# Fifteen projections of a two-layer hybrid decoder: three 256-column matmuls become one of 512 and one of 256, with some small TensorE work put together

## The chip, the cores and the metric

The kernel runs on one NeuronCore of a Trainium2 chip, in one launch. The metric is the device time of that launch in microseconds. The kernel before takes 1352.6 us, the median of three runs (1352.0 to 1353.1).

## The reference

Two layers, each `x <- LayerNorm(alpha * x + mixer(x))`, on x of 256 positions by 2048 channels, all in float32. Layer 0 has one input projection whose columns feed a Mamba-2 SSD mixer (xs, z, B, C, dt) and a block-sparse attention (q, k, v, gate); with 256 positions there is one block of 256 keys, so the attention is plain causal attention. Layer 1 is an S5 mixer: a projection to u and a gate, a diagonal complex scan over positions, a GLU, an output projection.

```python
def ssd_moba_mixer(x, w_in, ...):
    z, xbc, dt, q, k, v, gate = jnp.split(x @ w_in, SPLITS0, axis=-1)
    xbc = jax.nn.silu(causal_depthwise_conv(xbc, conv_w, conv_b))
    xs, bm, cm = jnp.split(xbc, ...)
    y = ssd_chunked_scan(xh * dt[..., None], dt * a, bm, cm)
    y = y + d_skip[:, None] * xh
    y_a = rms_norm(y * jax.nn.silu(z), norm_g)
    y_b = moba_attention(rope(q), rope(k), v) * jax.nn.silu(gate)
    return jnp.concatenate([y_a, y_b], axis=-1) @ w_out

def s5_mixer(x, w_in, ...):
    u, gate = jnp.split(x @ w_in, 2, axis=-1)
    y = jax.nn.gelu(s5_ssm(u, ...))          # scan over positions, 128 groups of 16 channels
    ga, gb = jnp.split(y @ w_glu, 2, axis=-1)
    return (ga * jax.nn.sigmoid(gb) * jax.nn.silu(gate)) @ w_out
```

## The kernel before

**Products.** Every large product is made from fp32r matmuls (one pass over float32 operands of reduced precision). To keep float32 accuracy each operand is split in a high and a low part, x = xh + xl and w = wh + wl, and three terms are summed in PSUM: wh·xh, wh·xl and wl·xh. The activations lie in SBUF as `xh` and `xl`, [128, 16 k-tiles, 256 positions], in slots called A and B (later C and F). The weights are streamed: one unit is 512 KB in a `raw` tile (two k-tiles of 512 columns, `_chunk`, L90). `split_to` (L209) issues its DMA on the SP queue, makes wh on ACT (L230) and wl on DVE (L232); four buffers of each, so a unit is split up to three units ahead of the one TensorE works on. A product of 512 output columns over 2048 rows is `CU` = 8 units.

**Two kinds.** `product` (L301) has kind "x", where a 128x128 piece of x is stationary and 512 weight columns move (`xmm`, L271, the matmul is L276), and kind "w", where a 128x128 piece of the weight is stationary and the 256 positions of x move (`wmm`, L280, the matmul is L297). Kind "w" leaves the output transposed (channels on partitions), which the conv, z, q, k, the gates and u need. A product owns two PSUM banks (`banks`, L267), and two products alternate between two pairs. In a "w" product the 512 output columns are four tiles of 128 (index o), two in each bank, and every tile takes three 256-column matmuls per k-tile (i = 0, 1, 2 in L297).

**The order of work.** After each unit, `pump` (L248) runs some of `jobs` (what the last product left to do) and of `back` (long-running work, spread over a number of units by `goal`). `run` (L242) places a job behind the weight split two units ahead, and a scheduler settles the order of each engine's queue when the program is built. Each engine then works in order. The products follow each other so: B and C together, xs (4 products), z (4), then four times q, k, v, gate, then the output projection of layer 0, u (4), the S5 gate (4), the GLU, the output projection.

**The work around the change.**
- `conv_jobs` (L523): for each tile of 128 channels one ACT operation and three DVE operations (L532) that read the product in PSUM, into an SBUF tile; then SiLU.
- z: SiLU on ACT from PSUM into `sz` (slot D), two jobs for each product (L853). The attention gates: the same into `sg`, L957. u: `u_store` (L1101) copies PSUM to the SBUF tile `ut` on ACT and sends it to DRAM on the POOL queue, from where the scan loads it again.
- `head_jobs` (L774): the SSD sums, for pairs of heads k = 0..15, in five steps: bcast (two TensorE matmuls, L782), decay (ACT), weigh (DVE), apply (TensorE, L812 and L813, float32, into half of a PSUM tile that two pairs share), comb (DVE, ACT, POOL). `skewed` runs step s of pair k in round k + s, the late steps first, so each round has the apply of one pair and the bcast of another.
- `block_jobs` (L662): the tables of the S5 scan, 16 blocks, as `back` work from v of the first head group on: bars, efs, fcs on DVE, `pes` (L709) with four transposes (L715) and eight small float32 matmuls (L719) on TensorE, and for every second block `mts` (L734).

Of the kernel before, what the change touches and what calls it, by code (L numbers as in the profile page):

```python
# [16 lines left out]
P = 128  # L17
S = 256
# [3 lines left out]
CU = KT // UK  # L22
ALPHA = 4.0 ** 0.25
# [70 lines left out]

def _layout(inp):
# [12 lines left out]
    cols = [xs, z]  # L108
    for h in range(4):
        cols += [m[:, 512 * h : 512 * h + 512] for m in (q, k, v, g)]  # L110
    b, c = _chunk(b), _chunk(c)
    first = np.stack([b[:PAIRED], c[:PAIRED]], 1).reshape(-1, P, UK * 512)
    a["wi0"] = np.concatenate([first, b[PAIRED:], c[PAIRED:]] + [_chunk(m) for m in cols], 0)
# [4 lines left out]
    a["wi1"] = _chunk(f["in1_w"][0])  # L118
# [44 lines left out]
def trunk(tc, io, out):  # L163
# [8 lines left out]
    with ExitStack() as top:  # L172
# [98 lines left out]
        def xmm(ps, o, wpair, j, hk, start, stop):  # L271
            (xh, xl), k = hk
            wh, wl = wpair
            sl = slice(o * P, o * P + P)
            for i, (l, r) in enumerate(((xh, wh), (xh, wl), (xl, wh))):
                T.matmul(ps[o], l[:, k, sl], r[:, j, :], start=start and i == 0, stop=stop and i == 2)  # L276
# [3 lines left out]
        def wmm(ps, u, nu, hl, wpair, parts=WHOLE):  # L280
            pv = [p.rearrange("p (f n) -> p f n", n=S) for p in ps]
            wh, wl = wpair
            for part in parts:
# [7 lines left out]
                for j, o in steps:  # L291
                    first, end = u == 0 and j == 0, u == nu - 1 and j == UK - 1
                    (xh, xl), k = hl(u * UK + j)
# [7 lines left out]
        def product(kind, hl, nu=CU, prelude=None, first=WHOLE):  # L301
# [15 lines left out]
            return ps  # L317

# [73 lines left out]
        xh = big("A", [P, KT, S], F32R)  # L392
        xl = big("B", [P, KT, S], F32R)
# [10 lines left out]
        with ExitStack() as l0:  # L404
# [35 lines left out]
            def xhl(k):  # L440
                return (xh, xl), k
# [81 lines left out]
            def conv_jobs(ps, ft, dst):  # L523
                acc = a4([P, 4, S])

                def tap(f):
                    def go():
                        src = ps[f // 2][:, (f % 2) * S : (f % 2) * S + S]
                        A.activation(acc[:, f, :], src, AF.Identity, bias=cb[:, ft + f : ft + f + 1], scale=cw[:, ft + f, 3:4])
                        for k in (2, 1, 0):  # L530
                            sh = 3 - k
                            V.scalar_tensor_tensor(acc[:, f, sh:], src[:, : S - sh], cw[:, ft + f, k : k + 1], acc[:, f, sh:],  # L532
                                                   op0=OP.mult, op1=OP.add)
# [11 lines left out]
            fmem = big("F", [P, 4096])  # L545
# [114 lines left out]
            ktp = [None]  # L660

            def block_jobs(b):  # L662
# [3 lines left out]
                def bars():  # L666
                    bc = h["bc"] = pp.tile([P, 4, 8, 16], F32, tag="bc", name=nm("bc"))
                    nc.sync.dma_start(bc.rearrange("p a g m -> p (a g m)"), io["s5bc"][b].rearrange("p a g m -> p (a g m)"))
                    bb = h["bb"] = pp.tile([P, 3, 8, 16], F32, tag="bb", name=nm("bb"))
# [10 lines left out]
                    V.tensor_scalar(bb[:, 2], bc[:, 2], nsg, None, op0=OP.mult)  # L680
# [7 lines left out]
                def efs():  # L688
                    bc, bb = h["bc"], h["bb"]
                    et = h["et"] = pp.tile([P, 8, 16, 4], F32, tag="et", name=nm("et"))  # L690
# [18 lines left out]
                def pes():  # L709
                    et, ob, bb = h["et"], h["ob"], h["bb"]  # L710
                    ev = et.rearrange("p (a i) m s -> p a (i m s)", i=2)
                    cv = bb[:, 2].rearrange("p (a i) m -> p a i m", i=2)
                    pe, pk = aux(), aux()
                    for a in range(4):
                        T.transpose(pe[:, a * P : a * P + P], ev[:, a, :], ident)  # L715
                    for a in range(4):
                        for i in range(2):
                            at = 64 * (i ^ (a % 2))
                            T.matmul(pk[at : at + 64, a * 16 : a * 16 + 16], ev[:, a, 64 * i : 64 * i + 64], cv[:, a, i, :], start=True, stop=True)  # L719
                    A.activation(ob[:, 0:512], pe, AF.Copy)  # L720
                    if b % 2 == 0:
                        ktp[0] = pp.tile([P, 8, 16], F32, tag="kt", name=nm("kt"))
                    kt = ktp[0][:, 4 * (b % 2) : 4 * (b % 2) + 4, :]
                    dc = PR("s5d")[:, 4 * b : 4 * b + 4].unsqueeze(2).to_broadcast([P, 4, 16])
                    V.tensor_tensor(kt, C("kmask").unsqueeze(1).to_broadcast([P, 4, 16]), dc, op=OP.mult)
                    V.tensor_tensor(kt, pk[:, 0:64].rearrange("p (a m) -> p a m", m=16), kt, op=OP.add)
                    nc.scalar.dma_start(wb[b][:, 0:1024], ob)
# [14 lines left out]
                return [bars, efs, fcs, pes, mts] if b % 2 else [bars, efs, fcs, pes]  # L742

            xs = big("C", [P, 2, D])
# [19 lines left out]
            for j in range(4):  # L764
                ps = product("w", xhl)
                xs_jobs(ps, j)

            sz = big("D", [P, KT, S])
# [5 lines left out]
            def head_jobs(k):  # L774
# [40 lines left out]
                def comb():  # L815
                    if k % 2 == 1:
                        sv = sz[:, k - 1 : k + 1, :].rearrange("p f n -> p (f n)")
                        V.tensor_tensor(sv, d["y"], sv, op=OP.mult)
                        jk = c2([P, 2, S])
                        A.activation(jk.rearrange("p f n -> p (f n)"), sv, AF.Square)  # L820
                        for f in range(2):
                            G.tensor_tensor(ssq, ssq, jk[:, f, :], op=OP.add)

                return [bcast, decay, weigh, apply, comb]
# [24 lines left out]
            for j in range(4):  # L849
                ps = product("w", xhl)  # L850
                for i in range(2):
                    fs = slice(4 * j + 2 * i, 4 * j + 2 * i + 2)
                    jobs.append(lambda ps=ps, i=i, fs=fs: A.activation(sz[:, fs, :].rearrange("p f n -> p (f n)"), ps[i], AF.Silu))  # L853
# [24 lines left out]
            def attn_jobs(g, qT, kT, v, sg):  # L878
                for hp in range(2):
# [37 lines left out]
                    def pv(hp=hp, hold=hold):  # L917
# [8 lines left out]
                        if not yb:  # L926
                            yb["h"] = big("C", [P, KT, S], F32R)
                            yb["l"] = big("F", [P, KT, S], F32R)
# [9 lines left out]
            for g in range(4):  # L938
# [9 lines left out]
                if g == 0:  # L948
# [6 lines left out]
                ps = product("w", xhl)  # L955
                sg = a4([P, 4, S])
                jobs.extend([lambda ps=ps, sg=sg, i=i: A.activation(sg[:, 2 * i : 2 * i + 2, :].rearrange("p f n -> p (f n)"), ps[i], AF.Silu)  # L957
                             for i in range(2)])
                attn_jobs(g, qT, kT, v, sg)

            yah = big("A", [P, KT, S], F32R)
            yal = big("B", [P, KT, S], F32R)
# [11 lines left out]
            def mixhl(k):  # L974
                if k < 12:
                    return (yb["h"], yb["l"]), k
                if k < 28:
                    return (yah, yal), k - 12
                return (yb["h"], yb["l"]), k - 16

            def tailhl(k):
                return ((yb["h"], yb["l"]), k) if k < 16 else ((yah, yal), k - 16)
# [30 lines left out]
        with ExitStack() as lt:  # L1013
# [22 lines left out]
            def turned(t, f0, nf):  # L1036
                if not x1t:
                    x1t["h"] = big("C", [P, KT, S], F32R)
                    x1t["l"] = big("F", [P, KT, S], F32R)
# [42 lines left out]
            def x1hl(k):  # L1082
                return (x1t["h"], x1t["l"]), k
# [6 lines left out]
        with ExitStack() as l1:  # L1090
# [10 lines left out]
            def u_store(ps, j):  # L1101
                ut = w1("ut", [P, 4, S], 1)
                for i in range(2):
                    A.activation(ut[:, 2 * i : 2 * i + 2, :].rearrange("p f n -> p (f n)"), ps[i], AF.Copy)
                nc.gpsimd.dma_start(ud[j].rearrange("g a c -> (g a c)").rearrange("(f p t) -> p f t", p=P, t=S), ut)
# [115 lines left out]
            def y_split(j):  # L1221
                if j == 0:
                    y5["h"] = big("A", [P, KT, S], F32R)
                    y5["l"] = big("B", [P, KT, S], F32R)
# [23 lines left out]
            def y5hl(k):  # L1248
                return (y5["h"], y5["l"]), k

            y2h = big("C", [P, KT, S], F32R)
            y2l = big("F", [P, KT, S], F32R)
# [24 lines left out]
            def y2hl(k):  # L1277
                return (y2h, y2l), k
# [7 lines left out]
        with ExitStack() as l2:  # L1286
            tp = l2.enter_context(tc.tile_pool(name="tp2", bufs=1))
            keep[0], keep[1] = tp, range(unit[0] + 2 * CU, unit[0] + 3 * CU)
            gb1 = big("A", [P, 2, D])
# [55 lines left out]
```

## Time and profile before

| what | time or share |
|---|---|
| median of 3 runs | 1352.6 us |
| the profiled execution, its own time | 1355.75 us |
| its span, first to last instruction | 1353.9 us |
| ACT_TABLE_LOAD of one ACT group in it | 1283 ns each |
| HBM read / written | 260.41 MB / 20.97 MB |
| mean DMA rate over the span | 208 GB/s |

The profile's page has the busy time of each engine, the span in 40 slices, the DMA queues, the chain of work that ended last and the costliest groups of instructions. A matmul's recorded length is modelled and runs on into the next ones, so on TensorE (PE) the distance from one start to the next is what counts; the weight loads (PEld) run beside the matmuls. Other views list who waited for whom, the instructions in order of time, and the engines' busy time in stretches of the span.

### The profile page before, as it was taken

The numbers are of one execution on the slowest core, as the hardware profiler recorded it, in microseconds if no ns is written. First come the engines' busy times: TensorE is split into PE (matmuls) and PEld (weight loads), VectorE is DVE, ScalarE is ACT, GpSimd is POOL, SyncE is SP. The second block draws the span as 40 slices with busy tenths as digits, with TensorE's granted clock in tenths as the row PEclk, the third lists the DMA queues.
The fourth block names the chain that finished last, engine by engine and source line by source line (L and its number), as shares of the span: only waits on it lengthen the run. The fifth ranks groups of instructions, "written<-read, shape, count | busy, mean of one in ns | idle before, by whom it ended". The sixth has DMA issues, their size and how long they took to land.

```text
span 1353.9 us, 24904 instructions
## 1 busy us (share of the span) xinstructions
PE 1337.0 (99%) x9839; PEld 1205.5 (89%) x9839; DVE 981.2 (72%) x1560; ACT 673.0 (50%) x870; POOL 364.8 (27%) x648
## 2 busy tenths in 40 slices
PE   9999999999999999999999999999999999999996
PEld 8999999998998998998988888899988888888885
DVE  5767856787687879689787766748889856555556
ACT  5566567764544553554554334334444545444441
POOL 0041000122026528616798500022343100000001
PEclk9999999999999999999999999999999999999998
DMA  8655555545546756856767778497989766666762
GB/s 313 192 171 176 173 171 158 157 143 178 175 135 207 254 163 203 269 160 206 232 206 243 232 232 302 136 300 223 318 275 326 217 211 189 187 196 188 250 214 81
DMA packets 80741, 283.01 MB, mean 209 GB/s; under 512 B 9840, under 2 KB 12528, under 8 KB 80112
## 3 DMA queue, kind: packets, MB, share of 16 engines
q1 hardware_dynamic: 68112, 239.33, 56.2%
q0 software_dynamic: 7328, 30.42, 6.5%
q10 hardware_dynamic: 5184, 11.67, 2.3%
q8 instruction: 77, 1.26, 0.4%
q14 instruction: 40, 0.33, 0.1%
HBM read 260.41 MB, written 20.97 MB: 208 GB/s over the span
## 4 chain that ended last, share of the span: by engine, by line
PE 93%; DVE 4%; DMA 2%; issue 1%; ACT 0%; POOL 0%; SPq 0%; POOLq 0%; ACTq 0%; DVEq 0%
PE main L276 43%; PE main L297 42%; DVE wl L232 1%; PE aux L381 1%; PE aux L812 1%; PE aux L719 1%; PE enc L1149 1%; DMA bc<-in_s5bc 1%; PE dec L1194 1%; PE aux L924 1%; PE aux L892 1%; DMA ud<-ut 0%; PE aux L782 0%; PE dec L1190 0%; PE aux L715 0%
## 5 line engine op out<-in xcount | busy, mean ns | idle before, releaser
L232 DVE TENSOR_TENSOR wl<-raw,wh 128x1024 fp32r<-128x1024 f32 x431 | 538.4, 1251 | 323.4 <-ACT wh L230 317.4
L230 ACT ACTIVATE wh<-raw 128x1024 fp32r<-128x1024 f32 x431 | 455.8, 1059 | 580.3 <-PE main L276 269.2
L297 PE MATMUL main<-A,wh 128*128 128x256 f32 x1408 | 400.7, 285 | 1.3 <-ACT wh L230 1.1
L297 PE MATMUL main<-B,wh 128*128 128x256 f32 x1408 | 398.0, 284 | 0.0
L297 PE MATMUL main<-A,wl 128*128 128x256 f32 x1408 | 394.5, 283 | 0.0
L297 PEld LDWEIGHTS main<-A,wh 128*128 128x128 f32 x1408 | 269.7, 192 | 3.0 <-ACT wh L230 1.3
L297 PEld LDWEIGHTS main<-B,wh 128*128 128x128 f32 x1408 | 269.8, 192 | 0.4
L297 PEld LDWEIGHTS main<-A,wl 128*128 128x128 f32 x1408 | 267.8, 192 | 0.2 <-issue 0.2
L276 PE MATMUL main<-wl,A 128*128 128x512 f32 x512 | 200.5, 392 | 0.5 <-DVE wl L232 0.5
L276 PE MATMUL main<-wh,A 128*128 128x512 f32 x512 | 200.5, 392 | 0.0
L276 PE MATMUL main<-wh,B 128*128 128x512 f32 x512 | 199.9, 390 | 0.0
L276 PE MATMUL main<-wh,C 128*128 128x512 f32 x384 | 150.7, 393 | 0.0
L276 PE MATMUL main<-wh,F 128*128 128x512 f32 x384 | 149.8, 390 | 0.0
L276 PE MATMUL main<-wl,C 128*128 128x512 f32 x384 | 149.7, 390 | 0.0
L276 PEld LDWEIGHTS main<-wl,A 128*128 128x128 f32 x512 | 96.2, 188 | 21.3 <-DVE wl L232 1.8
L276 PEld LDWEIGHTS main<-wh,B 128*128 128x128 f32 x512 | 96.2, 188 | 19.9
L276 PEld LDWEIGHTS main<-wh,A 128*128 128x128 f32 x512 | 96.1, 188 | 19.8 <-issue 0.2
L653 POOL TENSOR_TENSOR c<-c 128x8 f32<-128x8 f32 (+2 forms) x192 | 106.7, 574 | 25.5 <-DMA wb<-c 18.0
L276 PEld LDWEIGHTS main<-wh,F 128*128 128x128 f32 x384 | 72.1, 188 | 15.3
L276 PEld LDWEIGHTS main<-wh,C 128*128 128x128 f32 x384 | 72.1, 188 | 15.1
L276 PEld LDWEIGHTS main<-wl,C 128*128 128x128 f32 x384 | 72.1, 188 | 14.6
L873 POOL TENSOR_TENSOR a<-a,b 64x512 f32<-64x512 f32 x16 | 28.2, 1769 | 169.1 <-DVE b L872 132.1
(279 smaller groups left out, 1651.6 us busy)
## 6 DMA issues: line engine op xcount, KB each, us to landing
raw<-in_wi SPq DMA_DIRECT2D x271, 512.0 KB, 4.0
raw<-in_wo SPq DMA_DIRECT2D x96, 512.0 KB, 4.3
raw<-in_wglu SPq DMA_DIRECT2D x64, 512.0 KB, 3.6
wt<-wb POOLq DMA_DIRECT2D x16, 896.0 KB, 6.9
wb<-ob ACTq DMA_DIRECT2D x16, 512.0 KB, 5.8
bc<-in_s5bc SPq DMA_DIRECT2D x16, 256.0 KB, 4.6
wb<-c POOLq DMA_DIRECT2D x16, 256.0 KB, 3.4
wb<-om ACTq DMA_DIRECT2D x16, 128.0 KB, 4.3
```

The source lines that it names most:

```text
L230: high = A.activation(wh, raw, AF.Copy)
L232: splits[n] = (loaded[-1], high, V.tensor_tensor(wl, raw, wh.bitcast(F32), op=OP.subtract))
L276: T.matmul(ps[o], l[:, k, sl], r[:, j, :], start=start and i == 0, stop=stop and i == 2)
L297: T.matmul(pv[o // 2][:, o % 2, :], l[:, j, sl], r[:, k, :], start=first and i == 0 and o % 2 == 0, stop=end and i == 2 and o % 2 == 1, sk ...
L381: end = T.transpose(dst[:, i * P : i * P + P], s, ident)
L653: G.tensor_tensor(p[:, :, :, 0:m], cs[:, :, :, 1 : m + 1], cs[:, i, :, n : n + 1].unsqueeze(1).to_broadcast([P, 2, 4, m]), op=OP.mult)
L719: T.matmul(pk[at : at + 64, a * 16 : a * 16 + 16], ev[:, a, 64 * i : 64 * i + 64], cv[:, a, i, :], start=True, stop=True)
L812: T.matmul(yo, xs[:, 0, xc], df[:, i, 0:256], start=True, stop=False)
L873: turns.append(G.tensor_tensor(q[0:64], q[0:64], tm, op=OP.add))
L892: T.matmul(px[:, 128:384], qT[:, h, P:S], kT[:, h, :], start=True, stop=True)
L924: T.matmul(po, v[:, 0, hs], pT[:, i, 0:256], start=True, stop=False)
L1149: T.matmul(px[64 * at : 64 * at + 64, i, r * 128 + q * 64 : r * 128 + q * 64 + 64], wt[64 * i : 64 * i + 64, a * P + 64 * r : a * P + 64 * ...
```

## The change

A new function, `product_wide`, takes the place of `product("w", ...)` for xs, z, the four attention gates and u products 1 to 3 (15 products). The high and low x now lie side by side in one tile, [128, 16, 2, 256] (`duo`), so that one matmul of 512 moving columns multiplies wh by both; its two halves of the PSUM bank hold wh·xh and wh·xl. A second matmul of 256 columns adds wl·xh to the second half. A bank then holds one tile of 128 channels, so a product runs in two halves of 256 output columns, each with two banks and four units; the weights of these products are laid out in units of four k-tiles of 256 columns (`_half`). At the end of each half, `total` copies the first half of the bank to SBUF on ACT and adds the second half on DVE, for each of two tiles. The SiLU of z and the gates then works in place on 1024 columns in SBUF, one job for a product; the taps of xs read the sum in SBUF (in `sz`, which z overwrites later); u is stored from the sum. q, k, B, C, the first u product and all of kind "x" keep their matmuls.

The slots A and B become one tile, and so do C and F (the table of C·B for the SSD sums, in F before, takes the upper half of C). Two smaller parts: the apply of an even head pair moves one round later, into the round of the odd pair's apply, and the rounds between have bcast alone; `pes` runs for two blocks at once (eight transposes, then sixteen small matmuls, and one set of two DVE operations instead of two).

```diff
+def _half(w):
+    k, n = w.shape
+    return w.reshape(k // (HK * P), HK, P, n // S, S).transpose(3, 0, 2, 1, 4).reshape(-1, P, HK * S)
...
+        def product_wide(hl, dst, then):
+            for h in range(2):
+                ps = banks()
+                for u in range(HU):
+                    split_to(unit[0] + 3)
+                    wh, wl = (w.rearrange("p a n -> p (a n)").rearrange("p (k n) -> p k n", k=HK) for w in ready.pop(unit[0]))
+                    steps = [(j, o) for o in range(2) for j in range(HK)] if u == HU - 1 else [(j, o) for j in range(HK) for o in range(2)]
+                    for j, o in steps:
+                        first, end = u == 0 and j == 0, u == HU - 1 and j == HK - 1
+                        (xh, xl, xx), k = hl(u * HK + j)
+                        sl = slice(o * P, o * P + P)
+                        T.matmul(ps[o], wh[:, j, sl], xx[:, k, :, :].rearrange("p a n -> p (a n)"), start=first, stop=False, skip_group_check=True)
+                        T.matmul(ps[o][:, S : 2 * S], wl[:, j, sl], xh[:, k, :], start=False, stop=end, skip_group_check=True)
+                    unit[0] += 1
+                    pump(2 * HU - 1 - HU * h - u)
+
+                def total(o, ps=ps, h=h):
+                    to = dst()[:, 2 * h + o, :]
+                    A.activation(to, ps[o][:, 0:S], AF.Copy)
+                    V.tensor_tensor(to, to, ps[o][:, S : 2 * S], op=OP.add)
+
+                for o in range(2):
+                    run(lambda o=o: total(o))
+                then(h)
...
+        def duo(tag):
+            t = big(tag, [P, KT, 2, S], F32R)
+            return t[:, :, 0, :], t[:, :, 1, :], t
...
                 def pes():
...
+                    pair = [(b - 1, pend.pop()), (b, h)]
+                    pk = aux()
...
+                    for n, (k, d) in enumerate(pair):
+                        pe = aux()
...
+                        transpose4(pe, [ev[:, a, :] for a in range(4)])
+                        A.activation(d["ob"][:, 0:512], pe, AF.Copy)
+                        nc.scalar.dma_start(wb[k][:, 0:1024], d["ob"])
+                    for n, (k, d) in enumerate(pair):
...
+                                T.matmul(pk[at : at + 64, 64 * n + a * 16 : 64 * n + a * 16 + 16], d["ev"][:, a, 64 * i : 64 * i + 64], cv[:, a, i, :], start=True, stop=True)
...
-                return [bars, efs, fcs, pes, mts] if b % 2 else [bars, efs, fcs, pes]
+                return [bars, efs, fcs, pes, mts] if b % 2 else [bars, efs, fcs, lambda: pend.append(h)]
...
             for j in range(4):
-                ps = product("w", xhl)
-                xs_jobs(ps, j)
+                raw = sz[:, 4 * j : 4 * j + 4, :]
+                product_wide(xhl, lambda raw=raw: raw, lambda h: None)
+                xs_jobs(raw, j)
...
-                return [bcast, decay, weigh, apply, comb]
+                return [bcast, decay, weigh, apply, comb] if k % 2 else [bcast, decay, weigh, lambda: None, apply]
...
-                ps = product("w", xhl)
-                for i in range(2):
-                    fs = slice(4 * j + 2 * i, 4 * j + 2 * i + 2)
-                    jobs.append(lambda ps=ps, i=i, fs=fs: A.activation(sz[:, fs, :].rearrange("p f n -> p (f n)"), ps[i], AF.Silu))
+                zs = sz[:, 4 * j : 4 * j + 4, :]
+                product_wide(xhl, lambda zs=zs: zs, lambda h, zs=zs: jobs.append(lambda: A.activation(zs, zs, AF.Silu)) if h else None)
...
-                ps = product("w" if j < 4 else "x", x1hl) if j else first1
-                if j < 4:
-                    jobs.append(lambda ps=ps, j=j: u_store(ps, j))
+                if j in range(1, 4):
...
+                    product_wide(x1hl, ut, lambda h, ut=ut, j=j: jobs.append(lambda: u_store(ut(), j)) if h else None)
+                    continue
+                ps = product("x", x1hl) if j else first1
```

More of the change, by code (lines that the diff above doesn't have):

```diff
@@ L22 @@
 CU = KT // UK
+HK = 4
+HU = KT // HK
 ALPHA = 4.0 ** 0.25
@@ L720, in pes @@
[L720 to L726, printed above, removed]
@@ L954, in trunk @@
                     goal[0] = unit[0] + 13 * CU + 6 * CU
-                ps = product("w", xhl)
                 sg = a4([P, 4, S])
-                jobs.extend([lambda ps=ps, sg=sg, i=i: A.activation(sg[:, 2 * i : 2 * i + 2, :].rearrange("p f n -> p (f n)"), ps[i], AF.Silu)
-                             for i in range(2)])
+                product_wide(xhl, lambda sg=sg: sg, lambda h, sg=sg: jobs.append(lambda: A.activation(sg, sg, AF.Silu)) if h else None)
                 attn_jobs(g, qT, kT, v, sg)
-            yah = big("A", [P, KT, S], F32R)
-            yal = big("B", [P, KT, S], F32R)
+            yah, yal, yax = duo("A")
             def ya_job(i):
```

114 lines of the change are left out of this document (61 added, 53 removed).

## The prediction

> **What bounds the kernel now.** I read the page first, then the waits, then the chain of work that ended last, then single stretches in order of time. The page:
>
> ```profile
> span 1353.9 us, 24904 instructions
> PE 1337.0 (99%) x9839; PEld 1205.5 (89%) x9839; DVE 981.2 (72%) x1560; ACT 673.0 (50%) x870; POOL 364.8 (27%) x648
> ...
> PE 93%; DVE 4%; DMA 2%; issue 1%; ACT 0%; POOL 0%; SPq 0%; POOLq 0%; ACTq 0%; DVEq 0%
> ```
>
> TensorE is busy 99% of the span and holds 93% of the chain. Its busy time alone proves little, since recorded matmuls overlap, so I look at what it waits for (who waited for whom, TensorE's rows; us, times, longest):
>
> ```profile
> PE main L297 <- DVE F L1048: 1.3, 1, 1.3
> PE enc L1149 <- DMA um<-ud: 1.3, 1, 1.3
> PE main L297 <- ACT wh L230: 1.1, 1, 1.1
> ...
> PE main L276 <- DVE wl L232: 0.5, 2, 0.3
> ```
>
> No wait is over 1.3 us. The weight splits, the heaviest work of DVE, make it wait 0.5 us in the whole run. TensorE's stream is the bound, and a nanosecond taken from it counts in full until something else is late.
>
> **The wide products.** The chain of waits has long stretches of one kind of matmul (start, us, what):
>
> ```profile
> 148.06 23.03 PE main L297 x192
> ...
> 1155.37 21.81 PE main L276 x96
> ```
>
> 256 columns take 23.03/192 = 0.1199 us, 512 columns 21.81/96 = 0.2272 us. Doubling the columns adds 0.1073 us, so each matmul pays 0.1199 - 0.1073 = 0.0126 us whatever its width. Before, a k-tile and a tile of 128 channels cost 3 x 0.1199 = 0.3597 us; after, 0.2272 + 0.1199 = 0.3471 us. The columns streamed stay 768: what goes is one fixed part. It is tempting to read 22% off a change from three matmuls to two, or off the chain's shares; the row gives 3.5%. There are 15 products x 16 k-tiles x 4 tiles = 960 such triples: 960 x 0.0126 = **12.1 us**.
>
> Before has no stream that alternates 512 and 256 columns. The nearest alternation is the dt product, 256 columns with weights of 64 and 32 columns by turns, 32 matmuls from the first row here to the last:
>
> ```profile
> 75.60 0.28 PE L453 MATMUL aux<-A,wdp 128*64 128x256 f32 x1
> 75.71 0.28 PE L454 MATMUL aux<-B,wdp 128*32 128x256 f32 x1
> ...
> 79.26 0.28 PE L297 MATMUL main<-A,wl 128*128 128x256 f32 x1
> ```
>
> (79.26 - 75.60)/32 = 0.1144 us for 256 columns. If the short matmul of the new pair ran so, the pair would be 0.3416 us and the gain 960 x 0.0181 = 17.4 us. At the other end the pair takes as long as the triple and the gain is nothing; a loss I exclude, since every column and every weight load that stays was there before. I take 12.1: the weights here are 128 columns wide, as in the 23.03 us row, and a matmul's spacing in both rows holds one weight load for each matmul, as in the new stream.
>
> The Trainium skill (TensorE: Matmul & The Clock Gate, Back-to-back issue gap) gives a warm matmul N/2.4 + 2.5 ns, 109 ns for 256 columns and 216 for 512; dropping one of three would then be worth 2.5 ns, an estimate of 2.4 us in all, where the rows here (120 and 227 ns) make it 12.1. The rows decide, but the page speaks against this change, and it returns as a rival.
>
> **The sums after each half.** Each of 60 tiles adds an ACT copy and a DVE addition of 256 columns. Prices from the groups:
>
> ```profile
> L1263 DVE TENSOR_TENSOR p<-main,gt 128x256 f32<-128x256 f32 x16 | 6.0, 415 | 0.5 <-ACT gt L1261 0.5
> ...
> L788 ACT ACTIVATE b<-aux,cums 128x256 f32<-128x256 f32 x32 | 15.0, 469 | 0.4 <-POOL a L873 0.4
> ```
>
> DVE gets 60 x 0.415 = 24.9 us, ACT 60 x 0.469 = 28.1 us, less the copies and SiLUs that now read sums (u's copies fall away for three products). Taps that read SBUF instead of PSUM: the nearest rows are
>
> ```profile
> L532 DVE SCALAR_TENSOR_TENSOR a<-main,params,a 128x255 f32<-128x255 f32 x24 | 10.9, 467 | 1.6 <-ACT a L529 1.6
> ...
> L795 DVE SCALAR_TENSOR_TENSOR b<-b,dts,F 128x256 f32<-128x256 f32 x32 | 16.7, 522 | 0.0
> ```
>
> so 48 taps may cost up to 48 x 0.055 = 2.6 us more on DVE. None of this is TensorE's. The cover is DVE's idle time in each product. The stretches of the fullest wide products (z 0, u 2, u 3; then one unchanged v for comparison; after the length: busy PE, PEld, DVE, ACT, POOL):
>
> ```profile
> 153.70:177.60 23.90, 23.90 (x202) 23.90 (x202) 22.59 (x57) 12.21 (x15) 0.00 (x0) 1.00 0.58 177
> ...
> 621.60:644.60 23.00, 23.00 (x118) 19.00 (x117) 22.81 (x39) 10.29 (x11) 13.45 (x25) 1.00 0.75 237
> ...
> 919.70:946.60 26.90, 26.90 (x387) 26.30 (x386) 23.20 (x34) 11.11 (x12) 9.24 (x17) 1.00 0.76 234
> 946.60:972.70 26.10, 26.10 (x355) 25.70 (x354) 21.91 (x32) 10.37 (x13) 11.49 (x20) 1.00 0.89 301
> ```
>
> A product gets 4 x 0.415 = 1.7 us of DVE and 64 x 0.0126 = 0.8 us less of TensorE. u 2: 24.9 of 26.1, u 3: 23.6 of 25.3; both fit. z 0: 24.3 of 23.1, 1.2 us too much; but the splits run three units ahead, 3 x 8 x 0.347 = 8.3 us, so a backlog of 1.2 us is not seen. The v stretch shows that DVE at 22.81 of 23.00 did not stop TensorE. The sum waits for TensorE's last matmul of the tile, and behind it in ACT's and DVE's queue stand the split of the unit three ahead and the last product's jobs. That split needs the buffer of the very unit that ends the half, so it could not start much earlier. The banks are wanted again four units later, 11 us. Still the queues get fuller: I put 1 us of new waits on TensorE, between 0 (everything covered) and 6 (0.1 us for each of 60 sums).
>
> **The larger rounds.** A visit of float32 matmuls costs more than its columns: entering, and going back to fp32r. bcast alone, then an apply visit, then two products of attention in one visit:
>
> ```profile
> 198.90 0.28 PE L297 MATMUL main<-A,wl 128*128 128x256 f32 x1
> 199.02 0.39 PE L782 MATMUL aux<-cumhl,sel 128*128 128x256 f32 x2
> 199.25 0.28 PE L297 MATMUL main<-A,wh 128*128 128x256 f32 x1
> ```
>
> ```profile
> 308.19 0.28 PE L297 MATMUL main<-A,wl 128*128 128x256 f32 x1
> 308.39 0.66 PE L812 MATMUL aux<-b,C 128*64 128x256 f32 x4
> 308.88 0.40 PE L813 MATMUL aux<-b,C 128*64 128x128 f32 x4
> 309.20 0.39 PE L297 MATMUL main<-A,wh 128*128 128x256 f32 x1
> 309.43 0.28 PE L297 MATMUL main<-B,wh 128*128 128x256 f32 x1
> ```
>
> ```profile
> 479.23 0.60 PE L924 MATMUL aux<-b,a 128*128 128x256 f32 x2
> 479.66 0.38 PE L925 MATMUL aux<-b,a 128*128 128x128 f32 x2
> 479.88 0.60 PE L924 MATMUL aux<-b,a 128*128 128x256 f32 x2
> ```
>
> bcast alone costs 199.25 - 198.90 - 0.12 = 0.23 us and needs no way back (sel and cumhl are fp32r). An apply visit costs 309.43 - 308.19 - 0.24 = 1.00 us, 0.11 of it behind the first matmul of main. A second apply in the same visit is the same columns as the attention pair, 479.88 - 479.23 = 0.65 us. Each apply put into another's visit saves 0.35 us. In the order in which the changed program issues its matmuls, visits with an apply go from 17 to 10: 7 x 0.35 = **2.5 us**. The tables:
>
> ```profile
> 403.75 0.28 PE L297 MATMUL main<-A,wl 128*128 128x256 f32 x1
> 403.87 0.60 PE L715 MATMUL aux<-consts,et 128*128 128x128 f32 x4
> 404.39 0.64 PE L719 MATMUL aux<-bb,et 128*64 128x16 f32 x16
> 404.97 0.39 PE L297 MATMUL main<-A,wh 128*128 128x256 f32 x1
> 405.19 0.28 PE L297 MATMUL main<-B,wh 128*128 128x256 f32 x1
> ```
>
> A visit is 405.19 - 403.75 - 0.24 = 1.20 us. Two in one save the way back of one; that is at least the 0.10 us behind the first main matmul and at most the 0.35 of the apply. I take 0.3, nearer the apply because here too the tile sizes change twice: 8 x 0.3 = **2.4 us**. Against it: after each attention gate there is now one SiLU job instead of two, so the two scores that shared a pump fall into two, four visits more in that order. At 0.25 each (inside the same bounds) that is **1.0 us**.
>
> **The sum**, against the profiled execution's own 1355.75 us, which is 3.15 over the median of the runs: -12.1 - 2.5 - 2.4 + 1.0 + 1.0 = -15.0, so 1340.75 there, **1337.6** as a median.
>
> **The rivals.**
> - *The fixed part stays* (chance 0.13): the next wide matmul's weights load under the short one, and if that load sets the pace the pair takes as long as the triple. For it: no row shows the mixture. Against it: in the 23.03 us row each load hides under 0.12 us. Without the 12.1 us: 1352.6 - 2.9 = 1349.7. The skill's gap above would end at the same place, an estimate of 1347.3.
> - *The short matmul runs at the dt product's pace* (0.12): 17.4 instead of 12.1 us, 1332.3. Against it: the weights there are narrow.
> - *DVE gets late in part* (0.09): in the order of the queues the sums push splits back where DVE is above 0.94 of a stretch. At 0.1 us for each of 60 sums, 6 us in place of 1: 1342.6.
> - *The sums become the bound* (0.07), the slower side: at the 30 ends of halves the lead of 8.3 us is gone, because DVE comes into them with a backlog, and TensorE stands for a copy and an addition, 0.469 + 0.415 = 0.88 us, each time: +26.5 instead of +1, 1363.1. It is slower than before from 16/30 = 0.53 us an end. Against it: 0.5 us of waits for wl in the whole run, and a v stretch at 0.99 without a stop.
>
> **How the numbers follow.** Forecast 0.59. Its own range, with 8 to 16 us for the pairs' part (inside 0 to 17.4) and 2 to 4 for the rounds: 1333 to 1343. To leave out no more than 2 in 10 it reaches to both neighbours: 1329 (17.4 us of pairs, 5 of rounds, no waits: 1330.2, and a little under) to 1350. Differences under 0.2%, 2.7 us, can hardly be told from none in this kernel, so faster means under 1349.9: the forecast, the second and third rival and half of the first, 0.59 + 0.12 + 0.09 + 0.06 = 0.86; no change the other half, 0.07; slower 0.07.
>
> **What would show it.** In the after profile: a long stretch of the new lines where pairs start 0.347 us apart (0.36 and the first rival holds, 0.342 and the second does); the wide matmuls 960 and the short ones 960; waits of main for wl and wh near the 1.6 us of before (over 10 and the last rival holds); a double apply near 1.65 us without bcast; DVE busy up by some 25 us and ACT up by less. The prediction is wrong if the mixture has a pace of its own, or if the ends of the halves show gaps.

## The result, and the profile after

The changed kernel takes 1341.57 us (median of 6 runs, 1340.59 to 1345.27) beside 1352.66 us for the kernel before in the same session. The ratio, here and below one of the means, is 0.9923 with a 95% interval of 0.9910 to 0.9936. The forecast was 1337.6. By the medians the gain is 11.1 us, about three quarters of the 15.0 that were worked out. The profiled execution of the changed kernel has 1342.95 us of its own.

First the page of the changed kernel: the span, the busy time of each engine, the chain's shares, and the groups of the new matmuls.

```profile
span 1341.1 us, 23054 instructions
PE 1322.8 (99%) x8879; PEld 1151.2 (86%) x8879; DVE 1002.0 (75%) x1604; ACT 685.9 (51%) x914; POOL 371.7 (28%) x648
...
PE 85%; DVE 6%; DMA 3%; POOL 2%; issue 2%; ACT 1%; SPq 0%; POOLq 0%; DVEq 0%; ACTq 0%
...
L339 PE MATMUL main<-A,wh 128*128 128x512 f32 x768 | 272.0, 398 | 0.0
L340 PE MATMUL main<-A,wl 128*128 128x256 f32 x768 | 215.6, 281 | 0.0
L339 PE MATMUL main<-C,wh 128*128 128x512 f32 x192 | 68.5, 401 | 0.0
```

TensorE has 960 matmuls fewer (9839 to 8879), and there are 768 + 192 = 960 long ones, as the forecast counted. It is still busy 99% of the span. DVE gained 20.8 us of work and ACT 12.9. The chain now leaves TensorE more often (85% in place of 93%), yet that is not lost time, as what TensorE waits for shows (who waited for whom; us, times, longest):

```profile
PE aux L550 <- DVE ew L536: 1.5, 1, 1.5
PE main L306 <- DVE C L1081: 1.3, 1, 1.3
PE main L306 <- ACT wh L239: 1.3, 1, 1.3
PE aux L424 <- DVE idle L419: 1.0, 1, 1.0
PE aux L774 <- DVE kt L767: 0.8, 1, 0.8
PE main L285 <- DVE wl L241: 0.5, 1, 0.5
PE main L306 <- ACT wh L231: 0.2, 1, 0.2
```

These are 6.6 us against 5.5 before. The waits for the weight splits (wh and wl) are 2.0 us against 1.9: the sums at the ends of the halves pushed no split back far enough to be seen. New are one wait for ew (softplus of dt) and one for kt (the tables of two blocks at once); the wait for um is gone.

Now the new stream itself, in order of time (start in us, recorded length, engine, line, what): a piece of an xs product, then a piece of the third attention gate, both of the changed kernel.

```profile
56.00 0.40 PE L339 MATMUL main<-A,wh 128*128 128x512 f32 x1
56.23 0.28 PE L340 MATMUL main<-A,wl 128*128 128x256 f32 x1
56.35 0.40 PE L339 MATMUL main<-A,wh 128*128 128x512 f32 x1
...
58.12 0.40 PE L339 MATMUL main<-A,wh 128*128 128x512 f32 x1
```

```profile
544.62 0.39 PE L339 MATMUL main<-A,wh 128*128 128x512 f32 x1
544.85 0.28 PE L340 MATMUL main<-A,wl 128*128 128x256 f32 x1
...
547.39 0.39 PE L339 MATMUL main<-A,wh 128*128 128x512 f32 x1
```

Six pairs take 58.12 - 56.00 = 2.12 us in the first, 0.353 us each. Eight pairs take 547.39 - 544.62 = 2.77 us in the second, 0.346 us each, which is the pace of the forecast (0.3471). The first is the usual one: apart from the third gate, the products lie between 348 and 353 ns a pair. Over the 15 products, the mean distance from a long matmul to the short one behind it is 234.7 ns, and from a short one to the long one behind it 116.7 ns: a pair takes **351.4 ns**. (These are neighbours with nothing between them; 21 distances just behind a visit of other matmuls, each longer by some 0.08 us or more, are left out, since they belong to the price of the visit.) The third gate alone keeps to 230 and 117 ns.

The visits that were put together, changed kernel, in order of time: two applies with the bcast of the next pair, then the tables of two blocks.

```profile
212.35 0.28 PE L340 MATMUL main<-A,wl 128*128 128x256 f32 x1
212.56 0.66 PE L853 MATMUL aux<-b,C 128*64 128x256 f32 x4
213.04 0.40 PE L854 MATMUL aux<-b,C 128*64 128x128 f32 x4
213.26 0.65 PE L853 MATMUL aux<-b,C 128*64 128x256 f32 x4
213.69 0.44 PE L854 MATMUL aux<-b,C 128*64 128x128 f32 x4
214.06 0.50 PE L823 MATMUL aux<-cumhl,sel 128*128 128x256 f32 x2
214.40 0.39 PE L339 MATMUL main<-A,wh 128*128 128x512 f32 x1
```

```profile
417.65 0.39 PE L285 MATMUL main<-wh,A 128*128 128x512 f32 x1
417.88 1.03 PE L415 MATMUL aux<-consts,et 128*128 128x128 f32 x8
418.84 1.11 PE L764 MATMUL aux<-cv,et 128*64 128x16 f32 x32
419.88 0.50 PE L285 MATMUL main<-wh,A 128*128 128x512 f32 x1
420.22 0.39 PE L285 MATMUL main<-wl,A 128*128 128x512 f32 x1
```

The first visit takes 214.40 - 212.35 - 0.12 = 1.93 us, 1.70 without the 0.23 of bcast (forecast: near 1.65). Two visits of 1.00 became one of 1.70, 0.30 saved. The second takes 420.22 - 417.65 - 2 x 0.227 = 2.12 us in place of two times 1.20: 0.28 saved.

The scores that had shared a visit: before, two together; after, one alone.

```profile
365.32 0.39 PE L891 MATMUL aux<-a,a 128*128 128x128 f32 x2
365.54 0.60 PE L892 MATMUL aux<-a,a 128*128 128x256 f32 x2
365.98 0.38 PE L891 MATMUL aux<-a,a 128*128 128x128 f32 x2
366.20 0.60 PE L892 MATMUL aux<-a,a 128*128 128x256 f32 x2
366.44 0.47 PE L297 MATMUL main<-A,wh 128*128 128x256 f32 x1
366.75 0.28 PE L297 MATMUL main<-B,wh 128*128 128x256 f32 x1
```

```profile
357.13 0.39 PE L929 MATMUL aux<-a,a 128*128 128x128 f32 x2
357.36 0.60 PE L930 MATMUL aux<-a,a 128*128 128x256 f32 x2
357.60 0.59 PE L306 MATMUL main<-A,wh 128*128 128x256 f32 x2
358.02 0.28 PE L306 MATMUL main<-A,wl 128*128 128x256 f32 x1
```

Together: 366.75 - 365.32 - 0.12 = 1.31 us. Alone: 358.02 - 357.13 - 2 x 0.12 = 0.65 us, and two of that are 1.30. Splitting them costs nothing. The first fence shows where the price of a way back went: the first score's second step lasts 365.98 - 365.54 = 0.44 us, the last score's 0.24, so it was paid inside the shared visit as well.

Last, the stretch of z 0 (length, then busy PE, PEld, DVE, ACT, POOL), and three groups of the changed kernel (the sum's two halves, and a tap that reads SBUF):

```profile
153.60:177.00 23.40, 23.40 (x138) 20.45 (x137) 22.01 (x52) 13.59 (x19) 0.00 (x0) 1.00 0.59 181
```

```profile
L347 DVE TENSOR_TENSOR D<-D,main 128x256 f32<-128x256 f32 x32 | 13.2, 411 | 0.2 <-ACT D L346 0.2
L569 DVE SCALAR_TENSOR_TENSOR a<-D,params,a 128x255 f32<-128x255 f32 x16 | 8.0, 502 | 0.0
...
L346 ACT ACTIVATE D<-main 128x256 f32<-128x256 f32 x32 | 12.0, 374 | 3.8 <-PE main L340 3.8
```

In z 0, DVE is at 22.01 of 23.40 us and TensorE never stops. The addition took 411 ns (forecast 415), the copy 374 (469).

One thing in the profile of before has to be taken off before the two executions are compared. In order of time, kernel before, just after the gap between the layers:

```profile
874.91 0.37 PE L297 MATMUL main<-C,wh 128*128 128x256 f32 x1
...
878.44 0.28 PE L297 MATMUL main<-C,wh 128*128 128x256 f32 x1
```

17 matmuls take 3.53 us, 0.208 us each instead of 0.120. Within that stretch the clock was granted at half, for about 3.4 us (874.94 to 878.36 us has a granted clock of 0.50), and 3.53 - 17 x 0.12 = 1.5 us were lost. The Trainium skill (TensorE: Matmul & The Clock Gate, Part 1) states that the gate judges activity in a free-running window of 3413 ns; the length here agrees. The profiled execution of the changed kernel has no such stretch. So the 12.8 us between the two spans (1353.9 and 1341.1) hold 1.5 us that are not the change, and 11.3 remain, close to the 11.1 between the medians.

### The profile page after: what moved, and what is told of

The parts are those of the page before. It is cut to its first block, busy times and chain, and to the rows that moved or that the text cites. A ratio compares the mean times of both kernels' runs of the same rounds, so it can differ in the third digit from the quotient of the medians.

```text
span 1341.1 us, 23054 instructions
## 1 busy us (share of the span) xinstructions
PE 1322.8 (99%) x8879; PEld 1151.2 (86%) x8879; DVE 1002.0 (75%) x1604; ACT 685.9 (51%) x914; POOL 371.7 (28%) x648
## 4 chain that ended last, share of the span: by engine, by line
PE 85%; DVE 6%; DMA 3%; POOL 2%; issue 2%; ACT 1%; SPq 0%; POOLq 0%; DVEq 0%; ACTq 0%
PE main L285 40%; PE main L306 17%; PE main L339 14%; PE main L340 7%; DVE wl L241 2%; PE aux L415 1%; DMA raw<-in_wi 1%; DMA xr<-in_xn 1%; DMA raw<-in_wo 1%; PE aux L853 1%; PE enc L1188 1%; ACT wh L239 1%; PE dec L1233 1%; PE aux L764 1%; PE aux L962 1%
## 5 line engine op out<-in xcount | busy, mean ns | idle before, releaser
L285 PE MATMUL main<-wh,A 128*128 128x512 f32 x1024 | 321.9, 392 | 0.0
L339 PE MATMUL main<-A,wh 128*128 128x512 f32 x768 | 272.0, 398 | 0.0
L285 PE MATMUL main<-wh,C 128*128 128x512 f32 x768 | 241.3, 392 | 0.0
L306 PE MATMUL main<-A,wh 128*128 128x256 f32 x1280 | 233.4, 286 | 1.6 <-ACT wh L239 1.3
L285 PEld LDWEIGHTS main<-wh,A 128*128 128x128 f32 x1024 | 191.9, 188 | 39.7 <-issue 0.3
L306 PEld LDWEIGHTS main<-A,wh 128*128 128x128 f32 x1280 | 198.6, 192 | 3.5 <-ACT wh L239 1.5
L339 PEld LDWEIGHTS main<-A,wh 128*128 128x128 f32 x768 | 144.4, 188 | 33.7
L285 PEld LDWEIGHTS main<-wh,C 128*128 128x128 f32 x768 | 144.0, 188 | 30.5
L339 PE MATMUL main<-C,wh 128*128 128x512 f32 x192 | 68.5, 401 | 0.0
L862 POOL TENSOR_TENSOR ssq<-ssq,c 128x256 f32<-128x256 f32 x16 | 15.3, 958 | 176.9 <-ACT c L860 176.2
```

Of the source, the lines that this page charges most:

```text
L306: T.matmul(pv[o // 2][:, o % 2, :], l[:, j, sl], r[:, k, :], start=first and i == 0 and o % 2 == 0, stop=end and i == 2 and o % 2 == 1, sk ...
L339: T.matmul(ps[o], wh[:, j, sl], xx[:, k, :, :].rearrange("p a n -> p (a n)"), start=first, stop=False, skip_group_check=True)
```

## The experiments

Ten of the twelve runs are of edited kernels; the changed kernel itself ran twice again, as "e_again" and "e_third". Each batch shared runs of the kernel before: 1353.34 us for the first four, 1352.55 for the next four, 1353.09 for the last four.

**What the long matmul is worth.** "e_three" keeps everything of the change but splits each 512-column matmul in two of 256:

```diff
-T.matmul(ps[o], wh[:, j, sl], xx[:, k, :, :].rearrange("p a n -> p (a n)"), start=first, stop=False, skip_group_check=True)
+T.matmul(ps[o][:, 0:S], wh[:, j, sl], xh[:, k, :], start=first, stop=False, skip_group_check=True)
+T.matmul(ps[o][:, S : 2 * S], wh[:, j, sl], xl[:, k, :], start=False, stop=False, skip_group_check=True)
```

> The changed kernel with the one 512-column matmul split again into two of 256 (wh by xh, wh by xl), everything else as changed: halves, sums, rounds. The changed kernel has 1341.6 us. Theory (the alternating stream of 512 and 256 columns runs at 0.353 us a pair, not 0.347): three of 256 take 0.360, so 960 x 0.0067 = 6.4 to 8.2 us come back, 1348 to 1350. Rival (the pair is worth the predicted 12.1 us, and what is missing was lost at the ends of the halves): 12.1 come back, 1353.7.

Measured: 1351.11 us (1349.90 to 1352.73), ratio 0.9985 [0.9976, 0.9994]. The changed kernel did not run in this batch; at its ratio of 0.9923 it would take 1342.9 us beside the same 1353.34. So the long matmuls are worth 8.2 us, give or take some 2 by the two intervals, and not 12.1; everything else in the change is worth 2.2 us together (forecast: 2.5 + 2.4 - 1.0 - 1.0 = 2.9). In order of time, e_three, twelve matmuls from the first row to the last:

```profile
204.92 0.28 PE L339 MATMUL main<-A,wh 128*128 128x256 f32 x1
...
206.36 0.28 PE L339 MATMUL main<-A,wh 128*128 128x256 f32 x1
```

1.44 / 12 = 0.120 us each, over all products 359.8 ns for three. So the halves, the banks and the order of the tiles leave the pace of 256 columns as it was.

**Whether the sums cost anything.** "e_double" makes each copy and each addition of a sum twice, with the same output:

```diff
-A.activation(to, ps[o][:, 0:S], AF.Copy)
-V.tensor_tensor(to, to, ps[o][:, S : 2 * S], op=OP.add)
+for _ in range(2):
+    A.activation(to, ps[o][:, 0:S], AF.Copy)
+    V.tensor_tensor(to, to, ps[o][:, S : 2 * S], op=OP.add)
```

> The changed kernel with each copy and addition of total done twice (24.9 us more on DVE, 28.1 us more on ACT, the same result). Theory (the sums are covered by idle time of ACT and DVE): within 2 us of 1341.6. Rival (DVE late in part, 0.1 us for each of 60 sums): 1346 to 1348. Rival (the sums stand in TensorE's way at each of 30 ends, 0.88 us): about 1368.

Measured: 1343.13 us, ratio 0.9928 [0.9916, 0.9941], and the same span as the changed kernel, 1341.1 us. DVE is busy 19.4 us longer (1021.4) and ACT 19.5 (705.4), and the time hardly moves; TensorE waits 2.5 us for the weight splits in place of 2.0. The sums are hidden, with as much room again.

**The two parts by themselves.** "e_rounds" is the kernel before with the larger rounds alone (the paired apply and the paired tables); "e_wide" is the changed kernel with the old rounds (shown are the lines that choose the steps of a round; the steps themselves go back with them):

```diff
-return [bars, efs, fcs, pes, mts] if b % 2 else [bars, efs, fcs, lambda: pend.append(h)]
+return [bars, efs, fcs, pes, mts] if b % 2 else [bars, efs, fcs, pes]
...
-return [bcast, decay, weigh, apply, comb] if k % 2 else [bcast, decay, weigh, lambda: None, apply]
+return [bcast, decay, weigh, apply, comb]
```

> The kernel before with the larger rounds alone (apply of even pairs one round later, tables two blocks at a time). Theory (a joined visit saves one way into float32 and back, 0.3 us, as the changed trace shows it: 2149 ns for two tables against two of 1215, and 2.2 us for the sums): 4 to 4.5 us below before. Rival (the saving in TensorE's order is lost to waits for DVE's tables, which now come two at a time): 0 to 2 us below before.

> The changed kernel with the old rounds (each apply in its own round, each block's tables by themselves). Theory (the alternating stream is worth 960 x 0.0085 = 8.1 us and the rest is the rounds'): 7 to 8.5 us below before, 3 to 4 above the changed kernel. Rival (wide matmuls and rounds share a saving, so that the parts do not add): within 1.5 of the changed kernel.

> The changed kernel itself, for a comparison on the same chip with the next three. All theories: 11 us below the kernel before (10 to 12).

Measured: e_rounds 1349.2 us, ratio 0.9971 [0.9961, 0.9981], 3.4 us below the kernel before, somewhat less than expected. e_wide 1347.25 (1345.78 to 1350.01), ratio 0.9961 [0.9948, 0.9975], 5.3 below, a miss (7 to 8.5 were expected). e_again 1343.27, ratio 0.9934 [0.9921, 0.9947], 9.3 below. The parts add up to 8.7 of 9.3, so within these intervals neither needs the other. The larger rounds are worth 3.4 us alone and 4.0 on top of the wide products. Why e_wide's runs stand higher than its pairs (352.1 ns) let expect isn't settled. Its profiled execution had a stretch of half clock too (granted clock 0.996, as in the profile of before, where the first profile of the changed kernel has 0.998), and between these two profiles the spans differ by 8.4 us (1345.5 and 1353.9), as expected. The clock alone doesn't explain the other runs: three of e_wide's five have 0.997 and take 1345.78 to 1348.16 us, while the two of e_again at 0.997 take 1343.21 and 1343.27, so they lie 2.5 to 5 us apart where 3 to 4 had been expected.

**Where the pace comes from.** In the first batch two kernels reorder the matmuls of a unit: "e_two" issues two long, then two short; "e_eight" eight long, then eight short (four and four in the last unit of a half). Only the groups differ (e_two: two steps in each); e_eight's are:

```diff
-for j, o in steps:
+groups = [steps[0:4], steps[4:8]] if u == HU - 1 else [steps]
+for group in groups:
+    for j, o in group:
...
+        T.matmul(ps[o], wh[:, j, sl], xx[:, k, :, :].rearrange("p a n -> p (a n)"), start=first, stop=False, skip_group_check=True)
+    for j, o in group:
...
+        T.matmul(ps[o][:, S : 2 * S], wl[:, j, sl], xh[:, k, :], start=False, stop=end, skip_group_check=True)
```

> The changed kernel with the matmuls of each unit in the order long, long, short, short instead of long, short, long, short. Theory (the alternation itself is what costs 6 ns a pair): half of the switches are gone, so part of the 960 x 0.006 = 5.8 us comes back, 1337 to 1340. Rival (the matmul over xh and xl together has a pace of its own, 0.233 to 0.241 us, whatever stands beside it): no change, 1341.6 within 1.

> The changed kernel with all eight long matmuls of a unit first and then all eight short ones. Theory (alternation): the long ones start 0.227 us apart and the short ones 0.120, a pair is 0.347, 5 to 6 us less than the changed kernel, 1335.5 to 1337. Rival (own pace of the long one): 0.235 + 0.117 as now, 1341.6 within 1. A third way: the last short of a unit needs wl later and the first long needs wh earlier, so if the splits were near, waits for wh would show; I expect none over 1 us.

Measured: e_two 1341.80, ratio 0.9915 [0.9902, 0.9927]; e_eight 1339.78 (1339.11 to 1340.71), ratio 0.9900 [0.9887, 0.9913]. Both miss their theory's range: e_two has the time of its rival, and e_eight lies between the two. Beside the 1342.9 us that the changed kernel would take in this batch, they gain 1.1 and 3.1 us. So the times of this batch don't decide between alternation and a pace of the long matmul's own; the distances do. In order of time, e_eight:

```profile
205.02 2.00 PE L341 MATMUL main<-A,wh 128*128 128x512 f32 x8
206.86 1.11 PE L346 MATMUL main<-A,wl 128*128 128x256 f32 x8
207.81 1.09 PE L341 MATMUL main<-A,wh 128*128 128x512 f32 x4
```

Eight long ones take 1.84 us (0.230 each), eight short ones 0.95 (0.119 each), 0.349 for a pair. Averaged over the whole run by their place in the row of eight, the distances behind the long ones are 233, 234, 231, 230, 230, 228, 227 and 227 ns. A long matmul just behind short ones takes 233 ns or so, and only the seventh in a row has the 227 ns of the forecast.

"e_snake" goes further and turns the order round in every second unit, so that rows of 16 meet:

```diff
+for kind in ("ls", "sl")[u % 2]:
+    for j, o in steps:
...
+        if kind == "l":
+            T.matmul(ps[o], wh[:, j, sl], xx[:, k, :, :].rearrange("p a n -> p (a n)"), start=first, stop=end, skip_group_check=True)
+        else:
+            T.matmul(ps[o][:, S : 2 * S], wl[:, j, sl], xh[:, k, :], start=False, stop=False, skip_group_check=True)
```

> The changed kernel with runs of 8 long, 16 short, 16 long and 8 short matmuls in each half (the units' order turns round every second time). Theory (a long matmul is stretched to 0.233 us only near a switch and comes back to 0.227 from the seventh of a run on, as with runs of eight): a pair of 0.348, 3 us less than the changed kernel. Rival (runs do not matter): as the changed kernel within 1. Rival (the splits are late, since a unit's wl is wanted first in every second unit): waits for wl on TensorE over 2 us in all and 1 to 3 us more than with runs of eight.

Measured: 1341.65 us, ratio 0.9917 [0.9903, 0.9930], 1.6 below e_again where about 3 had been expected; the two intervals overlap, so the time shows no more than a hint. Its pace is as expected, 348.4 ns a pair. In order of time, e_snake:

```profile
99.83 3.12 PE L341 MATMUL main<-A,wh 128*128 128x512 f32 x13
102.78 2.08 PE L343 MATMUL main<-A,wl 128*128 128x256 f32 x16
104.69 1.33 PE L341 MATMUL main<-A,wh 128*128 128x512 f32 x5
```

13 long ones in 2.95 us are 0.227 each, 16 short ones in 1.91 us 0.119 each: both kinds, once in a long row, have the pace of the rows of before.

"e_long" asks whether the long matmuls of this stream have a slow pace of their own. It makes the short one long too:

```diff
-T.matmul(ps[o][:, S : 2 * S], wl[:, j, sl], xh[:, k, :], start=False, stop=end, skip_group_check=True)
+T.matmul(ps[o], wl[:, j, sl], xx[:, k, :, :].rearrange("p a n -> p (a n)"), start=False, stop=end, skip_group_check=True)
```

> The changed kernel with the short matmul made a long one too (wl by both xh and xl, 512 columns; it adds the fourth term wl by xl, in the first half of the bank wh by xh + wl by xh, in the second wh by xl + wl by xl). Theory (a long matmul is stretched only by the short ones around it): all start 0.227 us apart, a pair 0.454, the time 1342 + 960 x 0.1026 = 1440. Rival (a matmul that moves xh and xl together has a pace of its own, or one that fills a whole bank here): 0.233 or more each, a pair 0.466 or more, 1452 or more.

Measured: 1439.8 us, ratio 1.0639, as the theory had it. In order of time, e_long, twelve matmuls from the first row to the last:

```profile
394.66 0.39 PE L340 MATMUL main<-A,wl 128*128 128x512 f32 x1
...
397.38 0.39 PE L340 MATMUL main<-A,wl 128*128 128x512 f32 x1
```

2.72 / 12 = 0.227 us each, with the same tiles, banks and weights. So the length alone isn't slow in these products, and by e_three the width of 256 isn't either: each width keeps its pace in a stream of its own, and it is the mixture that stretches the long one.

**Once more, beside each other.** e_two and e_eight ran again with the changed kernel:

> The changed kernel a third time, to stand beside the next two on one chip. All theories: 9 to 11 us below the kernel before.

> Long, long, short, short again, beside the changed kernel. From the traces' pairs (0.3487 us against 0.3514): 2.6 us less than the changed kernel. If the order is worth nothing: within 1 of it, on either side.

> Runs of eight long and eight short matmuls again, beside the changed kernel. From the traces' pairs (0.3496 us against 0.3514): 1.7 us less than the changed kernel. If the order of the matmuls is worth nothing: within 1 of it, on either side.

Measured: e_third 1343.04, ratio 0.9924 [0.9912, 0.9936]; e_two_b 1342.5, 0.9920 [0.9908, 0.9932]; e_eight_b 1340.7, 0.9906 [0.9892, 0.9920]. Eight by eight is 2.3 us under the changed kernel, a little more than expected, and all five of its runs lie under all six of the changed kernel (1339.17 to 1341.78 and 1341.91 to 1343.93), though the intervals of the ratios still touch. Two by two is 0.5 under it, a miss (2.6 were expected from its pairs). One wait tells the profiled executions apart. What TensorE waits for, e_two_b (its longest row):

```profile
PE aux L556 <- DVE ew L542: 2.3, 1, 2.3
```

Neither e_third nor e_eight_b has a row for ew. With the pairs and the sum of TensorE's waits, each profiled execution can be laid against the first one of the changed kernel (351.4 ns, 6.6 us, span 1341.1). The fourth column is 960 times the difference of the pairs, plus the difference of the waits, plus 1.5 us, as an estimate from the stretch above, where the granted clock is 0.996 in place of 0.997 or 0.998:

| kernel | pair, ns | waits, us | worked out, us | span, us | measured, us |
|---|---|---|---|---|---|
| e_two | 348.7 | 7.0 | -2.2 | 1338.8 | -2.3 |
| e_eight | 349.6 | 5.8 | -2.5 | 1338.7 | -2.4 |
| e_snake | 348.4 | 6.6 | -1.4 | 1339.7 | -1.4 |
| e_again | 351.4 | 7.3 | +2.2 | 1343.5 | +2.4 |
| e_third | 351.4 | 5.7 | +0.6 | 1341.4 | +0.3 |
| e_two_b | 348.7 | 7.7 | 0.0 | 1341.8 | +0.7 |
| e_eight_b | 349.6 | 5.0 | -1.8 | 1338.9 | -2.2 |
| e_double | 351.3 | 7.6 | +0.9 | 1341.1 | 0.0 |

Seven of eight agree within 0.7 us. The account is of single executions and can't show more than that. In the last batch e_two_b's profiled execution stood 2.3 us for ew, the changed kernel's beside it not at all, which would account for most of what its pairs gained; that its other runs waited as long is not shown (the profiled one, 1343.59, is the slowest of the five). That wait differs from one execution to the next: the changed kernel stood 1.5 us for it in its first profile and 1.6 in e_again. In the first batch e_two's span is 2.3 us shorter, as its pairs say, its median only some 1.1. There the two profiled executions stand on opposite sides of their medians: 1342.95 beside 1341.57 for the changed kernel, 1340.58 beside 1341.80 for e_two, the only one of its four runs with a granted clock of 0.998. e_eight has the lowest median of all versions that ran, in both batches.

## Why the prediction came out as it did

The mechanism was right in the main: TensorE's stream was the bound and still is, what the change takes off it counts in full, and the work it adds elsewhere is hidden. One step failed, and by the sign that the prediction had set for it: the mixture has a pace of its own, 351.4 ns a pair and not 347.1. Point by point:

- **The pairs, forecast 12.1 us: measured 8.2** (e_three against the changed kernel), and 960 x (0.3597 - 0.3514) = 8.0 from the distances. This is the term that was mis-sized, by 4 us, and it is all of the miss. The working took the pace of each width from a stream of that width alone, and allowed for a mixture only by the bounds of 0 and 17.4 us and by two rivals. In the mixture the short matmul is 3 ns faster than in its own stream (117 instead of 120), and the long one 8 ns slower (235 instead of 227). Of the 12.6 ns that a matmul less was to save, 4.3 are lost there, and 8.3 remain. The range for the pairs' part, 8 to 16 us, just held it; no row had given its lower end, so that it did was luck.
- **The first rival** (the fixed part stays, 1349.7) fails: pairs start 0.351 us apart, not 0.360, and e_three is 8.2 us slower. The Trainium skill's gap of 2.5 ns (TensorE: Matmul & The Clock Gate, Back-to-back issue gap, where it stands for an isolated matmul) would have left an estimate of 2.4 us; the 8.0 measured decide. **The second** (the dt product's pace, 0.3416) is right about the short matmul, which does run below 0.120, and wrong about the pair.
- **The sums, forecast hidden with 1.0 us of new waits**: the waits went from 5.5 to 6.6 us, but hardly by way of the splits, as the step had it (2.0 instead of 1.9): the new ones are ew and kt, and the wait for um, 1.3 us, is gone. That the sum, 1.1, met the forecast is luck: in e_third, the same kernel, all waits are 5.7 us. e_double shows the cover. Both rivals in which DVE gets late, the one that ends slower among them, fail by the same run.
- **The taps from SBUF**, 48 of them, were bounded at 2.6 us more on DVE, from 467 and 522 ns. The row above has 502 ns, and the taps of 254 and 253 columns have 551 and 501, beside 473 and 472 before: 518 on average, 2.3 us more for the 48. TensorE never waited for them; ACT did, 6.6 us for all taps in place of 3.7.
- **The apply rounds, forecast 2.5 us:** 7 x 0.30 = 2.1. **The tables, forecast 2.4:** 8 x 0.28 = 2.2. **The split scores, forecast +1.0:** 0; there the step took a price from visits whose parts save the way between them, and the scores, by the 0.44 and 0.24 us above, paid it inside the shared visit too. Together -4.3 instead of -3.9: three sizes were off, and that they nearly cancel is luck. As time, the rounds are worth 3.4 us alone and 4.0 on top of the wide products.

The sum with the measured terms is -8.0 - 2.1 - 2.2 + 0 + 1.1 = -11.2 us, beside -11.1 in the medians and -11.3 in the spans once the half clock of the profile of before is taken off. The forecast set its sum against that execution and took it over to the median as it was, which does no harm to a difference.

**What stays open:** why a long matmul behind a short one is stretched, by 6 to 8 ns, and needs about six more of its kind to recover; and why the third gate keeps to 0.346 us with the same order of matmuls that gives 0.353 elsewhere. It did so in all four profiles of the stream (the first, e_again, e_third and e_double), yet in e_wide, with the same matmuls and other visits around them, it takes 0.353 too. No run here takes the distance apart below a single matmul.

## What to carry to other kernels

Where the matmul stream is the bound, a fixed part for each instruction is worth as much as its count, but price a mixed stream by a mixed stream: two paces, each taken from a row of one kind, overstated this gain by half. If two widths must alternate, group them, eight and eight here, and look at what the new order makes wait. Before calling added work on the other engines a danger, double it once: that answers in one run what a page of queue reasoning can't.

## What the runs showed of the hardware

- A 512-column fp32r matmul takes 227 ns in a row of its kind (e_long, e_snake), 233 to 235 behind a short one (230 in one product of 15). By its place in the row it comes back to 227 only at the seventh (e_eight, e_snake); a 256-column matmul goes from 115 or 116 ns to 120 along its row.
- Whether float32 matmuls gain by sharing a visit depends on what is put together: two applies in one visit save 0.30 us and the tables of two blocks 0.28, two scores nothing.
- The clock can be granted at half for some 3.4 us in the middle of a run: 0.208 us instead of 0.120 for 17 matmuls, 1.5 us in all, in some executions of a program and not in others. Of the 14 profiles seven have such a stretch: five just behind the gap between the layers (before, e_again, e_wide, e_two_b, e_eight_b), one at 529.81 to 533.23 us (e_third) and one at 109.25 to 112.67 (e_snake), both in or just behind a visit of float32 matmuls.
